# Attention scores as three products of high and low parts, a value product with the values held still, and rotary tables made later, in a two-block network on one core

## The chip, the core and the metric

The program runs on one core of a Trainium2 chip, as one launch. Its engines are TensorE (PE: matrix products; PEld is its loading of the stationary operand), VectorE (DVE), ScalarE (ACT), GpSimd (POOL) and SyncE (SP, which issues most DMAs). The metric is the device time of one execution in microseconds (us), smaller is better.

## What is computed

The reference has two blocks on 256 latent tokens of width 1024, and 256 context tokens beside them in block 1. Everything is float32.

```
block 1, layers l = 0, 1:
    sh, sc, gt ... = ada_modulation(cond, w_ada[l], b_ada[l])
    p  = modulate(rms_norm(h)) @ w_in[l];  pc = the same for the context tokens
    y_a = differential attention: 4 heads; for both 64-wide halves m of a head
            s[m] = q[m] @ k[m].T / 8;  w = softmax(s[0]) - lam * softmax(s[1]);  o = w @ v (128 wide); rms_norm
    y_b = spatial gating
    y_c = neighbourhood attention: 8 heads of 64; window scores + bias and context scores,
            one softmax over both;  o = p @ v
    h  = h + gt1 * (sum over the 3 branches of sigmoid(gate) * (y @ w_branch)) @ w_out
    (layer 0 does all of this for the context tokens too)
    h  = h + gt2 * mixture of 32 experts, 2 a token
block 2:
    gated linear attention, short convolution, dilated attention (q and k rotated by cos/sin of
    positions * inverse frequencies), gated merge, then a feed-forward part
```

## The kernel before

A tile framework takes the program's operations in the order of the code, with their data dependences and buffers, and its scheduler lays down one list of instructions per engine; each engine then works its list in order. So an instruction that waits holds up all that stands behind it on its engine, and where an operation stands is decided when the program is built.

Dense layers take their weights from HBM (2 MB a load, issued by SP into buffers called `raw`), split each into a high part `wh` (ACT copy, L153) and a low part `wl` (DVE subtraction, L155) in the format fp32r, and form three products (`dense_x`: L247 to L249, activations `xh`, `xl` stationary; `dense_w`: L229 to L231, weights stationary). A product of f32 operands is two records of PE in the trace, one of fp32r operands is one.

One call of `mix` handles a layer. Rows of q and k are transposed (`T`, L137) so that features stand on partitions; `qT` and `kT` have 4 tiles of 128 features, and the two 64-row halves of such a tile are the two maps of one differential head, or two neighbourhood heads.

- Differential part: for each of the 128-token tiles `t` (4 in layer 0, 2 in layer 1) and each of 4 heads, two f32 score products (L618), each on its row half of PE; a chain of maximum (L621), exponential (L624), reciprocal and scaling (L626 to L629) on DVE and ACT; 4 or 2 transposes; an ACT copy to `wT` (the transposed weights); and the value product (L637).
- Neighbourhood part: for each tile and each pair of heads two f32 score products (L675), then per head bias and maximum (L689, L691), exponentials (L694, L696), transposes, copy to `wT` (L708) and the value product (L710) with `wT` stationary and 64 columns of v moving. The sum of the exponentials divides the result at the end (L713), and `to_yT` transposes that for the next dense layer (L137, tile `ytok`).

The latent tiles see 512 keys, the context tiles 256. In both parts `at` holds the tiles, with two buffers of `P`/`PC` and four of the tag `t2`; scores, transposes and value products go through the PSUM buffers `aux`. Between one head's scores and its transposes the scheduler puts dense products of the gates or of the modulation vectors of later stages (L361, the modulation products). `gate_branch` and `to_yT` follow.

`rope_tables` (L1336 and on) makes cosT and sinT of block 2 from the inverse frequencies and the positions; before, `idle` calls it at the program's start, behind the norm's scaling (L424), and a table load of ACT stands on either side of it (L1359, L1733). `mix2_consts` makes `sin2`, the table with its negative, and `ev_rope` uses both.

Of the kernel before, what the change touches and what calls it, by code (L numbers as in the profile page):

```python
# [89 lines left out]
class Builder:  # L90
# [173 lines left out]
    def setup(self, st, open_mix, load_x):  # L264
        nc, I = self.nc, self.I
# [6 lines left out]
        c = self.p_const  # L272
# [15 lines left out]
        with self.tp("setup", 1) as tp:  # L288
# [4 lines left out]
            inv = self.p_h.tile([128, 64], FT, name="inv2")  # L293
            nc.gpsimd.dma_start(inv, I["k_inv"])
            pi = self.p_h.tile([128, 2], I32, name="pi")
            nc.gpsimd.dma_start(pi, I["positions_2"][0].rearrange("(t p) -> p t", p=128))
            self.rope_in = inv, pi
# [110 lines left out]
    def mix_norm(self, tp, l, h, mid=None, junk=None, idle=None):  # L408
# [6 lines left out]
        for w in range(2):  # L415
            y = tp.tile([128, 2, D], FT, name="xs", tag="xs", bufs=2)
            r = self.stats(h, (2 * w, 2 * w + 1), y[:, 0] if junk is None else junk)
            if w == 0 and self.spare:
                self.fence.append(self.sq)
            for k in range(2):  # L420
                scaled = nc.vector.tensor_scalar(y[:, k], h[:, 2 * w + k], r[:, k:k + 1], None, op0=OP.mult)
            xs.append(y)
        if idle is not None:
            with self.tc.issue_after(scaled.ins):  # L424
                idle()
# [81 lines left out]
    def mix(self, l, xh, xl):  # L507
# [80 lines left out]
        rope = at.tile([128, 256], FT, name="rope")  # L588
        nc.gpsimd.dma_start(rope, I["k_rope"])

        def ev_qk(dst):
            def ev(t, ps):
# [8 lines left out]
                nc.scalar.activation(dst[:, :, t * 128:(t + 1) * 128], pt.rearrange("p (c t) -> p c t", c=4), AF.Copy)  # L601
# [5 lines left out]
        for t in tts:  # L607
# [4 lines left out]
            for h in range(4):  # L612
                S = [self.aux() for _ in range(2)]
                mx, nm, sm = (self.small(2, f"da{x}") for x in "xns")
                P = at.tile([128, 2, 512], FT, name="P", tag="P", bufs=2)
                for m in range(2):
                    r0 = m * 64
                    mm(S[m][:, :nk], lhsT=qT[r0:r0 + 64, h, t * 128:(t + 1) * 128], rhs=kT[r0:r0 + 64, h, k0:],  # L618
                       start=True, stop=True)
# [3 lines left out]
                for m in range(2):  # L623
                    nc.scalar.activation(P[:, m, :nk], S[m][:, :nk], AF.Exp, bias=nm[:, m:m + 1], scale=0.125,  # L624
                                         accum_out=sm[:, m:m + 1])
# [34 lines left out]
        self.dense_w(W(O_KC), 8, 512, xh, xl, 512, lambda c, ps: nc.scalar.activation(kT[:, c], ps, AF.Copy))  # L660
        self.dense_w(W(O_QC), 8, 512, xh, xl, n, lambda c, ps: nc.scalar.activation(qT[:, c, :n], ps[:, :n], AF.Copy))
        self.dense_x(W(O_VC), 8, 512, xh, xl, allt, lambda t, ps: nc.scalar.activation(v[:, t], ps, AF.Copy))
        yc = at.tile([128, 4, 512], FT, name="ytok", tag="ytok")
        for t in tts:
            po = self.aux()
            sm = self.small(8, "nsm")
# [3 lines left out]
            for h in range(8):  # L670
                c, r0 = h // 2, (h % 2) * 64
                if h % 2 == 0:
                    S2 = [self.aux() for _ in range(2)]
                    for m in range(2):
                        mm(S2[m][:, :nk], lhsT=qT[m * 64:m * 64 + 64, c, t * 128:(t + 1) * 128],  # L675
                           rhs=kT[m * 64:m * 64 + 64, c, k0:], start=True, stop=True)
                S = S2[h % 2]
                P = at.tile([128, 2, 512], FT, name="PC", tag="P", bufs=2)[:, 0]
                mx, nm, ps2 = (self.small(2, f"na{x}") for x in "xns")
                if lat:  # L680
                    if h % 2 == 0:
                        bt = at.tile([128, 2, 4, 64], FT, name="bt", tag="t2", bufs=4)
                        for u in range(2):
                            off = h * 889 + (3 - (2 * t + u)) * 127 + 63
                            for k in range(2):
                                nc.gpsimd.dma_start(bt[u * 64:(u + 1) * 64, k], bass.AP(
                                    tensor=self.d_bias.tensor, offset=self.d_bias[l].offset + off + k * 889,
                                    ap=[[7111, 64], [127, 4], [1, 64]]))
                    nc.vector.tensor_tensor_reduce(P[:, :256], S[:, :256], bt[:, h % 2].rearrange("p a b -> p (a b)"),  # L689
                                                   1.0, -3e38, OP.add, OP.max, mx[:, 0:1])  # L690
                    nc.vector.tensor_reduce(mx[:, 1:2], S[:, 256:], axis=AX.X, op=OP.max)  # L691
                    nc.vector.tensor_tensor(mx[:, 0:1], mx[:, 0:1], mx[:, 1:2], op=OP.max)
                    nc.vector.tensor_scalar(nm[:, 0:1], mx[:, 0:1], -0.125, None, op0=OP.mult)
                    nc.scalar.activation(P[:, :256], P[:, :256], AF.Exp, bias=nm[:, 0:1], scale=0.125,  # L694
                                         accum_out=ps2[:, 0:1])
                    nc.scalar.activation(P[:, 256:], S[:, 256:], AF.Exp, bias=nm[:, 0:1], scale=0.125,  # L696
                                         accum_out=ps2[:, 1:2])
                    nc.vector.tensor_tensor(sm[:, h:h + 1], ps2[:, 0:1], ps2[:, 1:2], op=OP.add)
                else:
                    nc.vector.tensor_reduce(mx[:, 0:1], S[:, :nk], axis=AX.X, op=OP.max)  # L700
                    nc.vector.tensor_scalar(nm[:, 0:1], mx[:, 0:1], -0.125, None, op0=OP.mult)
                    nc.scalar.activation(P[:, :nk], S[:, :nk], AF.Exp, bias=nm[:, 0:1], scale=0.125,
                                         accum_out=sm[:, h:h + 1])
                pt = self.aux()
                for b in range(nk // 128):
                    self.T(pt[:, b * 128:(b + 1) * 128], P[:, b * 128:(b + 1) * 128])
                wT = at.tile([128, 512], FT, name="wT", tag="t2", bufs=4)
                nc.scalar.activation(wT[:, :nk], pt[:, :nk], AF.Copy)  # L708
                for b in range(nk // 128):
# [1125 lines left out]
```

## Time and profile before

| | |
|---|---|
| median of 3 runs | 2613.09 us (2610.91 to 2614.15) |
| the profiled execution | 2611.69 us, its span 2609.9 us |
| PE, DVE, ACT busy over the span | 2471.3 (95%), 1309.2 (50%), 852.0 (33%) us |
| attention of layer 0, layer 1 | 183 to 560 us, 1285 to 1496 us |
| experts of layer 0, layer 1 | 700 to 1175 us, 1560 to 2010 us |
| block 2 | from about 2010 us |

A matrix product's record shows a start and a modelled length; since products are pipelined, the distance from one start to the next is the time that one takes, not the length shown. "x4" in a timeline is four records in a row, "[2.08 <-ACT PC]" is PE's idle time before it and what ended that.

### The profile page before, as it was taken

The numbers are of one execution on the slowest core, as the hardware profiler recorded it, in microseconds if no ns is written. First come the engines' busy times: TensorE is split into PE (matmuls) and PEld (weight loads), VectorE is DVE, ScalarE is ACT, GpSimd is POOL, SyncE is SP. The second block draws the span as 40 slices with busy tenths as digits, with TensorE's granted clock in tenths as the row PEclk, the third lists the DMA queues.
The fourth block names the chain that finished last, engine by engine and source line by source line (L and its number), as shares of the span: only waits on it lengthen the run. The fifth ranks groups of instructions, "written<-read, shape, count | busy, mean of one in ns | idle before, by whom it ended". The sixth has DMA issues, their size and how long they took to land. (4 is left out here: it accounts for less than half of the span.)

```text
span 2609.9 us, 33466 instructions
## 1 busy us (share of the span) xinstructions
PE 2471.3 (95%) x13560; PEld 1686.8 (65%) x13560; DVE 1309.2 (50%) x2640; ACT 852.0 (33%) x1504; POOL 163.2 (6%) x187
## 2 busy tenths in 40 slices
PE   7999999999889999997999978999898899998998
PEld 5766776677544444545878774444342798897997
DVE  5635523346444444548553463233232686657784
ACT  4334333424211111115444441111110534444663
POOL 1200002011200000003000210000000100001000
PEclk9999999999899999998999999999999999999999
DMA  9743544263889999985243478999999435535452
GB/s 316 214 162 114 169 146 122 93 209 149 329 342 417 419 417 418 418 356 193 73 133 104 139 300 328 421 421 421 421 421 413 164 119 194 177 122 184 152 188 99
DMA packets 177363, 652.47 MB, mean 250 GB/s; under 512 B 15174, under 2 KB 18778, under 8 KB 127666
## 3 DMA queue, kind: packets, MB, share of 16 engines
q1 hardware_dynamic: 169682, 626.97, 62.4%
q0 software_dynamic: 7520, 23.29, 3.0%
q8 instruction: 109, 1.79, 0.3%
q14 instruction: 52, 0.43, 0.0%
HBM read 644.42 MB, written 5.80 MB: 249 GB/s over the span
## 5 line engine op out<-in xcount | busy, mean ns | idle before, releaser
L155 DVE TENSOR_TENSOR wl<-raw,wh 128x1024 fp32r<-128x1024 f32 (+1 forms) x279 | 335.8, 1207 | 310.9 <-ACT wh L153 305.3
L966 PE MATMUL acc<-raw,xg 128*64 128x512 f32 x896 | 399.0, 596 | 19.6 <-DMA raw<-in_moe_w_up 10.1
L153 ACT ACTIVATE wh<-raw 128x1024 fp32r<-128x1024 f32 (+1 forms) x288 | 299.0, 1045 | 334.9 <-PE acc L248 167.3
L968 PE MATMUL acc<-raw,xg 128*64 128x512 f32 x896 | 399.2, 596 | 0.0
L247 PE MATMUL acc<-xh,wh 128*128 128x256 f32 (+1 forms) x1184 | 370.6, 315 | 0.0
L248 PE MATMUL acc<-xl,wh 128*128 128x256 f32 (+1 forms) x1184 | 369.5, 313 | 0.0
L249 PE MATMUL acc<-xh,wl 128*128 128x256 f32 (+1 forms) x1184 | 368.5, 312 | 0.1
L966 PEld LDWEIGHTS acc<-raw,xg 128*64 128x64 f32 x896 | 119.8, 137 | 273.4 <-issue 247.2
L247 PEld LDWEIGHTS acc<-xh,wh 128*128 128x128 f32 x1184 | 226.3, 192 | 28.1 <-issue 13.8
L248 PEld LDWEIGHTS acc<-xl,wh 128*128 128x128 f32 x1184 | 226.4, 191 | 15.8 <-issue 5.9
L249 PEld LDWEIGHTS acc<-xh,wl 128*128 128x128 f32 x1184 | 225.9, 191 | 11.7 <-issue 1.0
L229 PE MATMUL acc<-wh,xh 128*128 128x512 f32 x544 | 214.0, 394 | 5.0 <-DVE xh L441 2.5
L230 PE MATMUL acc<-wl,xh 128*128 128x512 f32 x544 | 213.6, 393 | 0.3 <-DVE wl L155 0.3
L231 PE MATMUL acc<-wh,xl 128*128 128x512 f32 x544 | 213.8, 394 | 0.0
L990 PE MATMUL acc<-raw,hT 128*64 128x512 f32 x472 | 209.8, 596 | 3.0 <-ACT hT L982 3.0
L992 PE MATMUL acc<-raw,hT 128*64 128x512 f32 x472 | 209.8, 596 | 0.0
L997 DVE TENSOR_TENSOR aux<-aux,g 128x512 f32<-128x512 f32 x128 | 83.3, 694 | 185.7 <-PE aux L1083 185.7
L1108 DVE SCALAR_TENSOR_TENSOR yl<-acc,ws,yh 128x512 fp32r<-128x512 f32 x64 | 48.0, 750 | 214.6 <-ACT yh L1107 214.6
L990 PEld LDWEIGHTS acc<-raw,hT 128*64 128x64 f32 x472 | 61.8, 137 | 122.7 <-issue 115.3
L982 ACT ACTIVATE hT<-aux 128x512 f32<-128x512 f32 x32 | 19.1, 598 | 332.3 <-PE aux L137 332.3
L229 PEld LDWEIGHTS acc<-wh,xh 128*128 128x128 f32 x544 | 102.4, 188 | 31.8 <-issue 3.7
L968 PEld LDWEIGHTS acc<-raw,xg 128*64 128x64 f32 x896 | 119.8, 137 | 0.0
(479 smaller groups left out, 4303.0 us busy)
## 6 DMA issues: line engine op xcount, KB each, us to landing
raw<-in_moe_w_gate SPq DMA_DIRECT2D x59, 2048.0 KB
raw<-in_moe_w_down SPq DMA_DIRECT2D x59, 2048.0 KB
raw<-in_moe_w_up SPq DMA_DIRECT2D x53, 2048.0 KB
raw<-in_w_in SPq DMA_DIRECT2D x42, 2048.0 KB
raw<-in_w_ada SPq DMA_DIRECT2D x22, 2048.0 KB
rawx<-in_moe_w_up SPq DMA_DIRECT2D x11, 2048.0 KB
raw<-in_w_branch SPq DMA_DIRECT2D x18, 1024.0 KB
raw<-in_w_gate SPq DMA_DIRECT2D x6, 2048.0 KB
```

The source lines that it names most:

```text
L153: nc.scalar.activation(hi, src, AF.Copy)
L155: eng.tensor_tensor(lo, src, hi.bitcast(FT), op=OP.subtract)
L229: mm(ps[t][:, :W], lhsT=a, rhs=wh[:, jj, :W], start=j == 0, stop=False)
L230: mm(ps[t][:, :W], lhsT=a, rhs=wl[:, jj, :W], start=False, stop=False)
L231: self.last_mm = mm(ps[t][:, :W], lhsT=b, rhs=wh[:, jj, :W], start=False, stop=j == J - 1)
L247: mm(ps[c][:, :n], lhsT=a, rhs=xh[:, j, :n], start=j == 0, stop=False)
L248: mm(ps[c][:, :n], lhsT=a, rhs=xl[:, j, :n], start=False, stop=False)
L249: mm(ps[c][:, :n], lhsT=b, rhs=xh[:, j, :n], start=False, stop=j == J - 1)
L966: mm(ps[0:64], lhsT=xg[:, j, a0:a0 + 64], rhs=wa(j), start=j == 0, stop=j == 7)
L968: mm(ps[64:128], lhsT=xg[:, j, b0:b0 + 64], rhs=wb(j), start=j == 0, stop=j == 7)
L990: mm(py[half][0:64], lhsT=hT[:, c, 0:64], rhs=da(c, half), start=c == 0, stop=c == 3)
L992: mm(py[half][64:128], lhsT=hT[:, c, 64:128], rhs=db(c, half), start=c == 0, stop=c == 3)
```

## The change

Four things are changed. The scores of both parts are no longer one f32 product: q and k are kept as high and low fp32r parts (`hilo`: ACT copy, DVE subtraction), and `scores` forms qh·kh, ql·kh and qh·kl, with the two row halves taking turns inside each product. A fence (`scored`) lets the scores of a head or pair issue only when the last exponential of the one before has been issued. In the neighbourhood part v is stationary (64 columns) and the 128 columns of `wT` move; the two heads of a pair write the lower and the upper 64 partitions of the result. The weights are divided by their sum before they are transposed, and the result needs no transposes; an ACT copy and `hilo` take their place. The rotary tables, their inputs and their ACT table load move from the start to block 2, behind the transposes of the linear attention's output; `sin2`'s two DVE operations become a third sine. And the scratch for descriptors of POOL's DMAs is given as 2048 (it was not given), which makes its ring shorter and leaves room for the new tiles.

```diff
         def attn_tiles():
-            return (at.tile([128, 4, 512], FT, name="qT", tag="qT"),
-                    at.tile([128, 4, 512], FT, name="kT", tag="kT"))
+            return [[at.tile([128, 4, k], FR, name=f"{x}{p}", tag=f"{x}{p}") for p in "hl"]
+                    for x, k in (("q", n), ("k", 512))]
 
+        scored = []
+        def scores(c, t, k0):
+            S = [self.aux() for _ in range(2)]
+            nk = 512 - k0
+            with ExitStack() as es:
+                if scored:
+                    es.enter_context(tc.issue_after(scored.pop().ins))
+                for i, (a, b) in enumerate(((0, 0), (1, 0), (0, 1))):
+                    for m in range(2):
+                        r = slice(m * 64, m * 64 + 64)
+                        mm(S[m][:, :nk], lhsT=qT[a][r, c, t * 128:(t + 1) * 128], rhs=kT[b][r, c, k0:],
+                           start=i == 0, stop=i == 2)
+            return S
...
-                nc.scalar.activation(dst[:, :, t * 128:(t + 1) * 128], pt.rearrange("p (c t) -> p c t", c=4), AF.Copy)
+                self.hilo(*(d[:, :, t * 128:(t + 1) * 128] for d in dst), pt.rearrange("p (c t) -> p c t", c=4))
...
-                S = [self.aux() for _ in range(2)]
+                S = scores(h, t, k0)
...
-                for m in range(2):
-                    r0 = m * 64
-                    mm(S[m][:, :nk], lhsT=qT[r0:r0 + 64, h, t * 128:(t + 1) * 128], rhs=kT[r0:r0 + 64, h, k0:],
-                       start=True, stop=True)
...
+                scored[:] = [e]
...
-        self.dense_w(W(O_KC), 8, 512, xh, xl, 512, lambda c, ps: nc.scalar.activation(kT[:, c], ps, AF.Copy))
+        ev = lambda dst, k: lambda c, ps: self.hilo(dst[0][:, c], dst[1][:, c], ps[:, :k])
+        self.dense_w(W(O_KC), 8, 512, xh, xl, 512, ev(kT, 512))
...
-            for h in range(8):
+            for c in range(4):
+                S2 = scores(c, t, k0)
...
+                    scored[:] = [e]
+                    nc.vector.reciprocal(ps2[:, 0:1], ps2[:, 0:1])
+                    nc.vector.tensor_scalar(P[:, :nk], P[:, :nk], ps2[:, 0:1], None, op0=OP.mult)
...
-                for b in range(nk // 128):
-                    mm(po[:, h * 64:(h + 1) * 64], lhsT=wT[:, b * 128:(b + 1) * 128],
-                       rhs=v[:, k0 // 128 + b, h * 64:(h + 1) * 64], start=b == 0, stop=b == nk // 128 - 1)
-            nc.vector.reciprocal(sm, sm)
-            nc.vector.tensor_tensor(yc[:, t].rearrange("p (h d) -> p h d", h=8), po.rearrange("p (h d) -> p h d", h=8),
-                                    sm[:, :, None].to_broadcast([128, 8, 64]), op=OP.mult)
+                for b in range(nb):
+                    for m in range(2):
+                        h = 2 * c + m
+                        mm(po[m * 64:m * 64 + 64, c * 128:(c + 1) * 128],
+                           lhsT=v[:, k0 // 128 + b, h * 64:(h + 1) * 64], rhs=wTs[m][:, b * 128:(b + 1) * 128],
+                           start=b == 0, stop=b == nb - 1)
+            nc.scalar.activation(yc[:, :, t * 128:(t + 1) * 128], po.rearrange("p (c q) -> p c q", c=4), AF.Copy)
...
-        yh, yl = self.to_yT(yc, n)
+        yh = self.p_y.tile([128, 4, n], FR, name="yh", tag="yh")
+        yl = self.p_y.tile([128, 4, n], FR, name="yl", tag="yl")
+        for c in range(4):
+            self.hilo(yh[:, c], yl[:, c], yc[:, c, :n])
...
-        self.sin2 = bp.tile([128, 2, 2, 64], FT, name="sin2")
-        nc.vector.tensor_scalar(self.sin2[:, :, 0], self.rope2[1], -1.0, None, op0=OP.mult)
-        nc.vector.tensor_copy(self.sin2[:, :, 1], self.rope2[1])
...
-        nc.scalar.activation(sinT, a, AF.Sin)
+        nc.scalar.activation(sinT[:, :, 1], a, AF.Sin)
+        nc.scalar.activation(sinT[:, :, 0], a, AF.Sin, scale=-1.0)
...
+        cosT, sinT = self.rope_tables(dl, self.inv, self.pos)
...
-                def idle():
-                    self.rope2 = self.rope_tables(hp, *self.rope_in)
-
-                    nc.scalar.activation(hp.tile([128, 1], FT, name="tab"), self.rope2[0][:, 1, 0:1], AF.Tanh)
...
-    nc = bacc.Bacc("TRN2", target_bir_lowering=False, num_devices=1)
+    nc = bacc.Bacc("TRN2", target_bir_lowering=False, num_devices=1, dynamic_dma_scratch_size=2048)
```

The first place is PE's list in the differential part of layer 0: P is a head's weights, which `glob` (it holds the identity) transposes, `vv` the values, kT and qT the keys and queries, `acc` a dense product. Before:

```order
L249 MATMUL acc<-xh,wl 128x512
L137 MATMUL aux<-glob,P 128x128 x4
L618 MATMUL aux<-kT,qT 128x512
L637 MATMUL aux<-vv,wT 128x128 x4
L618 MATMUL aux<-kT,qT 128x512
L247 MATMUL acc<-xh,wh 128x512
```

After, at the same head, with the parts kh, kl, qh, ql:

```order
L249 MATMUL acc<-xh,wl 128x512
L137 MATMUL aux<-glob,P 128x128 x4
L593 MATMUL aux<-kh,qh 128x512 x2
L593 MATMUL aux<-kh,ql 128x512 x2
L642 MATMUL aux<-vv,wT 128x128 x4
L593 MATMUL aux<-kl,qh 128x512 x2
L247 MATMUL acc<-xh,wh 128x512
```

Two score products with the value product between them have become six, in a group of four and a group of two, around the same value product.

The second place is PE's list in the neighbourhood part of layer 0 (PC is a head's weights). Before:

```order
L137 MATMUL aux<-glob,PC 128x128 x2
L675 MATMUL aux<-kT,qT 128x512
L710 MATMUL aux<-vv,wT 128x64 x4
L675 MATMUL aux<-kT,qT 128x512
L710 MATMUL aux<-vv,wT 128x64 x4
L249 MATMUL acc<-xh,wl 128x512
```

After:

```order
L137 MATMUL aux<-glob,PC 128x128 x4
L721 MATMUL aux<-wT,vv 64x128
L593 MATMUL aux<-kh,qh 128x512 x2
L593 MATMUL aux<-kh,ql 128x512
L721 MATMUL aux<-wT,vv 64x128 x7
L593 MATMUL aux<-kh,ql 128x512
L593 MATMUL aux<-kl,qh 128x512 x2
L249 MATMUL acc<-xh,wl 128x512
```

The value products of a pair stand as one and seven, and the scores of the next pair as three and three around the seven.

The third place is PE's list at the end of the neighbourhood part of layer 1. Before (the first three rows are the last of 29 dense products in a row):

```order
L247 MATMUL acc<-xh,wh 128x256
L248 MATMUL acc<-xl,wh 128x256
L249 MATMUL acc<-xh,wl 128x256
L137 MATMUL aux<-glob,PC 128x128 x4
L710 MATMUL aux<-vv,wT 128x64 x4
L137 MATMUL aux<-glob,PC 128x128 x2
L137 MATMUL aux<-glob,ytok 128x128
```

After:

```order
L249 MATMUL acc<-xh,wl 128x256
L137 MATMUL aux<-glob,PC 128x128 x8
L721 MATMUL aux<-wT,vv 64x128
L593 MATMUL aux<-kh,qh 128x512
L721 MATMUL aux<-wT,vv 64x128 x7
L593 MATMUL aux<-kh,qh 128x512
L593 MATMUL aux<-kh,ql 128x512 x2
L593 MATMUL aux<-kl,qh 128x512 x2
L137 MATMUL aux<-glob,PC 128x128 x8
L721 MATMUL aux<-wT,vv 64x128 x8
L247 MATMUL acc<-yh,wh 128x256 x4
```

The last pair's scores now come behind the dense products, with no dense product between them and the last pair's transposes, and the transposes of the result (ytok) are gone.

## Rows read from the trace of the kernel before

**Rows 1.** Stretches: start:end, length, busy us (records) by engine, PEclk, DMA share, GB/s.

```profile
180.00:270.00 90.00, 89.15 (x408) 54.70 (x408) 49.92 (x126) 37.75 (x93) 1.50 (x3) 1.00 0.30 103
380.00:480.00 100.00, 99.65 (x487) 64.19 (x486) 35.78 (x123) 41.57 (x106) 16.37 (x27) 1.00 0.36 110
700.00:1175.00 475.00, 465.04 (x2377) 227.18 (x2374) 212.29 (x394) 57.23 (x92) 0.00 (x0) 0.99 0.97 399
1480.00:1500.00 20.00, 16.18 (x85) 13.15 (x84) 6.73 (x21) 7.96 (x20) 4.48 (x7) 0.77 0.55 173
2120.00:2290.00 170.00, 169.97 (x1029) 151.32 (x1028) 111.29 (x162) 77.71 (x98) 0.00 (x0) 1.00 0.51 171
```

**Rows 2.** Waits of PE, whole span: tile <- releaser: us, times, longest.

```profile
PE aux L137 <- ACT PC L694: 2.9, 3, 2.1
PE aux L137 <- DVE P L629: 2.5, 7, 0.6
```

**Rows 3.** Lines L675 (scores) and L710 (values): records, ns min/median/max, forms.

```profile
L675 PE MATMUL aux<-kT,qT x96: 376/589/694, 382.7 to 1482.7; 64*128 64x512 f32 x64, 64*128 64x256 f32 x32
L710 PE MATMUL aux<-vv,wT x320: 217/275/473, 388.8 to 1495.7; 128*128 128x64 f32 x160
```

**Rows 4.** PE's timeline, a pair of row halves: start, us, line, names, form, records.

```profile
183.38 1.13 PE L618 MATMUL aux<-kT,qT 64*128 64x512 f32 x4
```

**Rows 5.** PE's timeline, one row half alone.

```profile
200.32 0.72 PE L637 MATMUL aux<-vv,wT 128*128 128x128 f32 x5
200.97 1.12 PE L618 MATMUL aux<-kT,qT 64*128 64x512 f32 x2
202.03 0.50 PE L247 MATMUL acc<-xh,wh 128*128 128x512 f32 x1
202.36 0.39 PE L248 MATMUL acc<-xl,wh 128*128 128x512 f32 x1
202.59 0.39 PE L249 MATMUL acc<-xh,wl 128*128 128x512 f32 x1
```

**Rows 6.** PE's timeline, value product of the neighbourhood part.

```profile
412.91 2.00 PE L710 MATMUL aux<-vv,wT 128*128 128x64 f32 x16
414.84 1.12 PE L675 MATMUL aux<-kT,qT 64*128 64x512 f32 x2
```

**Rows 7.** Timeline, a pair of column halves in the expert part (PEld loads weights).

```profile
1667.28 0.59 PE L966 MATMUL acc<-rawx,xg 128*64 128x512 f32 x1
1667.28 0.14 PEld L966 LDWEIGHTS acc<-rawx,xg 128*64 128x64 f32 x1 [0.29 <-issue]
1667.28 0.59 PE L968 MATMUL acc<-rawx,xg 128*64 128x512 f32 x1
...
1667.70 0.59 PE L966 MATMUL acc<-rawx,xg 128*64 128x512 f32 x1
```

**Rows 8.** PE's timeline, from scores to transposes, differential part of layer 1.

```profile
1346.36 0.50 PE L247 MATMUL acc<-xh,wh 128*128 128x512 f32 x1
...
1350.69 0.63 PE L137 MATMUL aux<-glob,P 128*128 128x128 f32 x4
```

**Rows 9.** Timeline, end of the neighbourhood part of layer 1.

```profile
1486.52 0.28 PE L248 MATMUL acc<-xl,wh 128*128 128x256 f32 x1
...
1486.64 0.28 PE L249 MATMUL acc<-xh,wl 128*128 128x256 f32 x1
...
1488.35 0.50 ACT L694 ACTIVATE PC<-PC,nan 128x256 f32<-128x256 f32 x1
...
1494.17 1.97 PE L710 MATMUL aux<-vv,wT 128*128 128x64 f32 x8 [0.47 <-ACT wT L708]
...
1497.91 0.78 PE L247 MATMUL acc<-yh,wh 128*128 128x256 f32 x2
```

**Rows 10.** Timeline, modulation part at the start.

```profile
17.16 3.11 PE L361 MATMUL acc<-raw,condT 128*32 128x512 f32 x16
...
20.53 0.58 ACT L366 ACTIVATE part<-acc 128x512 f32<-128x512 f32 x1
```

More of the change, by code (lines that the diff above doesn't have):

```diff
@@ L406, in stats, with mix_norm @@
         return self.rsqrt(ss, 1.0 / D, EPS)
-    def mix_norm(self, tp, l, h, mid=None, junk=None, idle=None):
+    def mix_norm(self, tp, l, h, mid=None, junk=None):
         nc = self.nc
@@ L420, in mix_norm @@
             for k in range(2):
-                scaled = nc.vector.tensor_scalar(y[:, k], h[:, 2 * w + k], r[:, k:k + 1], None, op0=OP.mult)
+                nc.vector.tensor_scalar(y[:, k], h[:, 2 * w + k], r[:, k:k + 1], None, op0=OP.mult)
             xs.append(y)
-        if idle is not None:
-            with self.tc.issue_after(scaled.ins):
-                idle()
         order = [(w, j) for w in range(2) for j in range(0, 8, 2)]
@@ L712, in mix @@
-            nc.vector.reciprocal(sm, sm)
-            nc.vector.tensor_tensor(yc[:, t].rearrange("p (h d) -> p h d", h=8), po.rearrange("p (h d) -> p h d", h=8),
-                                    sm[:, :, None].to_broadcast([128, 8, 64]), op=OP.mult)
-            self.dump(f"yc{l}", lambda o: o[t * 128:(t + 1) * 128], yc[:, t])
+            nb = nk // 128
+            for c in range(4):
+                S2 = scores(c, t, k0)
+                if lat:
+                    bt = at.tile([128, 2, 4, 64], FT, name="bt", tag="t2", bufs=4)
+                    for u in range(2):
+                        off = 2 * c * 889 + (3 - (2 * t + u)) * 127 + 63
+                        for k in range(2):
+                            nc.gpsimd.dma_start(bt[u * 64:(u + 1) * 64, k], bass.AP(
+                                tensor=self.d_bias.tensor, offset=self.d_bias[l].offset + off + k * 889,
+                                ap=[[7111, 64], [127, 4], [1, 64]]))
+                wTs = []
+                for m in range(2):
+                    S = S2[m]
+                    P = at.tile([128, 2, 512], FT, name="PC", tag="P", bufs=2)[:, 0]
+                    mx, nm, ps2 = (self.small(2, f"na{x}") for x in "xns")
+                    if lat:
+                        nc.vector.tensor_tensor_reduce(P[:, :256], S[:, :256], bt[:, m].rearrange("p a b -> p (a b)"),
+                                                       1.0, -3e38, OP.add, OP.max, mx[:, 0:1])
+                        nc.vector.tensor_reduce(mx[:, 1:2], S[:, 256:], axis=AX.X, op=OP.max)
+                        nc.vector.tensor_tensor(mx[:, 0:1], mx[:, 0:1], mx[:, 1:2], op=OP.max)
+                        nc.vector.tensor_scalar(nm[:, 0:1], mx[:, 0:1], -0.125, None, op0=OP.mult)
+                        nc.scalar.activation(P[:, :256], P[:, :256], AF.Exp, bias=nm[:, 0:1], scale=0.125,
+                                             accum_out=ps2[:, 0:1])
+                        e = nc.scalar.activation(P[:, 256:], S[:, 256:], AF.Exp, bias=nm[:, 0:1], scale=0.125,
+                                                 accum_out=ps2[:, 1:2])
+                        nc.vector.tensor_tensor(ps2[:, 0:1], ps2[:, 0:1], ps2[:, 1:2], op=OP.add)
+                    else:
+                        nc.vector.tensor_reduce(mx[:, 0:1], S[:, :nk], axis=AX.X, op=OP.max)
+                        nc.vector.tensor_scalar(nm[:, 0:1], mx[:, 0:1], -0.125, None, op0=OP.mult)
+                        e = nc.scalar.activation(P[:, :nk], S[:, :nk], AF.Exp, bias=nm[:, 0:1], scale=0.125,
+                                                 accum_out=ps2[:, 0:1])
+                    scored[:] = [e]
+                    nc.vector.reciprocal(ps2[:, 0:1], ps2[:, 0:1])
+                    nc.vector.tensor_scalar(P[:, :nk], P[:, :nk], ps2[:, 0:1], None, op0=OP.mult)
+                    pt = self.aux()
+                    for b in range(nb):
+                        self.T(pt[:, b * 128:(b + 1) * 128], P[:, b * 128:(b + 1) * 128])
+                    wT = at.tile([128, 512], FT, name="wT", tag="t2", bufs=4)
+                    nc.scalar.activation(wT[:, :nk], pt[:, :nk], AF.Copy)
+                    wTs.append(wT)
+                for b in range(nb):
+                    for m in range(2):
+                        h = 2 * c + m
+                        mm(po[m * 64:m * 64 + 64, c * 128:(c + 1) * 128],
+                           lhsT=v[:, k0 // 128 + b, h * 64:(h + 1) * 64], rhs=wTs[m][:, b * 128:(b + 1) * 128],
+                           start=b == 0, stop=b == nb - 1)
@@ L1336, in rope_tables @@
     def rope_tables(self, rp, inv, pi):
-        nc, I, c = self.nc, self.I, self.p_const
-        cosT = c.tile([128, 2, 64], FT, name="cosT")
-        sinT = c.tile([128, 2, 64], FT, name="sinT")
+        nc = self.nc
+        cosT = rp.tile([128, 2, 64], FT, name="cosT")
+        sinT = rp.tile([128, 2, 2, 64], FT, name="sinT")
         pf = rp.tile([128, 2], FT, name="pf")
```

59 lines of the change are left out of this document (10 added, 49 removed).

## The prediction, made before the changed kernel ran

> **What bounds the kernel now.** I read the table of stretches first, then PE's waits, then the two score and value lines, and last the timelines around them. In the stretches the reader is to see that PE has next to no idle time while the attention runs: 89.15 of 90 us and 99.65 of 100 us, with DVE at about half and ACT at 40% [rows 1]. The waits say the same from the other side: over the whole program PE waits 2.9 and 2.5 us for the two softmax chains [rows 2]. So dense products of other stages cover the softmax, and what a stage there costs is the sum of what PE does in it: time taken out of PE's list shortens it one for one, as long as the chain stays covered. The experts are another case: DMA share 0.97 and 399 GB/s over 475 us [rows 1]. They wait for weights, but these are loaded into the buffers that the attention and its gates still hold, and in the attention the DMA is idle two thirds of the time (share 0.30 and 0.36 [rows 1]), so the weight stream starts earlier when the attention ends earlier, and the gain is kept.
>
> **What the rows price.** A record of an f32 product with 512 columns takes 0.42 to 0.43 us (start to start, 1667.28 to 1667.70 [rows 7]), a product has two, so 0.853. An fp32r product of 512 columns takes 0.23 (202.36 to 202.59 [rows 5]; 0.2275 over longer runs), one of 256 columns 0.12 (1486.52 to 1486.64 [rows 9]). Two row halves that stand next to each other run at once: four records last 1.13 us [rows 4], two records of one half alone last 1.12 [rows 5].
>
> Going into a row half and out of it costs. The half alone holds PE from 200.97 to 202.03, 1.06, which is 0.853 and 0.2; the five value records of 128 columns before it take 0.65, where a quarter of 0.4275 each would make 0.53, 0.1 too much; the first dense product behind it takes 0.33 instead of 0.23 [rows 5]. That is 0.4 for a group, 0.2 for each of its two boundaries. [...]
>
> **Scores.** Each of the two lines has 64 records at 512 columns and 32 at 256 [rows 3], together 64 products of 512 and 32 of 256. In PE's order of before, 24 of the 512 stand in 12 pairs and 40 alone, of the 256 also 12 pairs and 8 alone. So PE holds 52 turns of 0.853 and 20 of 0.427 (half): 44.4 + 8.5 = 52.9 us. After, there are three times as many products, 288, in 90 groups of one to six; two halves in a group share a turn, which gives 107 turns at 512 and 54 at 256: 107 × 0.2275 + 54 × 0.12 = 24.3 + 6.5 = 30.8. That is −22.1. No row of before shows fp32r on row halves. If they run one after the other, it is 192 × 0.2275 + 96 × 0.12 = 55.2, +2.3. I take the first, since f32 halves run at once in [rows 4] and the format is not what places them.
>
> **Value product of the neighbourhood part.** 320 records [rows 3], sixteen in 1.93 us [rows 6], 0.1206 each: 38.6 us. After, 160 f32 products of 128 moving columns with 64 stationary ones, in two column halves. Column halves of f32 run at once in the experts: both start at 1667.28 and the next at 1667.70 [rows 7]. A record of 128 columns takes a quarter of that 0.4275, 0.107; I take 0.112, near the 0.12 that records with a 128-column load reach. By the order (runs of one and seven, eight, three) the 160 make 101 turns: 101 × 0.224 = 22.6, −16.0. If the halves don't share a turn, it is 160 × 0.224 = 35.8, −2.8.
>
> **Transposes and boundaries.** 24 transposes of the result go (16 in layer 0, 8 in layer 1), at about 0.12: −2.9. In exchange ACT copies and splits the result; that work falls where dense products of gate 1 stand, except in layer 1 (below). About 29 changes between dense products and transposes go, since the transposes now stand as four, and some score groups beside modulation products: −2. The boundaries into and out of split groups rise from 144 to 206, as the value products are now split as well and stand between the scores: 62 × 0.2 = +12.4; it can be nothing where two kinds of split follow each other, so between 0 and 12.4, and I take it whole.
>
> PE's list becomes 22.1 + 16.0 + 2.9 + 2 − 12.4 = 30.6 us shorter, 30.
>
> **Waits that it adds.** The fence lets a pair's scores issue only behind the last exponential of the pair before. What is queued behind waiting scores is PE's whole list, the dense products too. In the differential part the scores stand behind the transposes anyway, which need that exponential; between scores and transposes PE has 21 to 23 dense products of 512 columns, 4.8 to 5.2 us, while the chain took 4.33 us (1346.36 to 1350.69 [rows 8]) with one maximum already at work; with both behind the scores it is some 0.6 longer. So it is just covered; +1 in all. In the neighbourhood part of layer 0 the latent pairs have 26 to 30 dense products, 5.9 to 6.8 us, and the chain gets two more DVE operations for a head, +1.5; the context pairs have 8 to 12, 1.8 to 2.7 us, for a chain with one exponential: +2 over eight pairs.
>
> At the end of layer 1 the last pair has no cover. [...] From the first exponential to the second head's value product it took 5.82 us (1488.35 to 1494.17 [rows 9]). After, the dense products stand ahead of the last pair's scores and cover the pair before by 3.4 of its 6, and the last pair's chain runs bare: about 0.9 for its maxima, 5.8, 0.9 for the new scaling and 3 for values, copy and split, 10.6 where it was 11.2, and 2.5 to 3.5 for the pair before, less the ytok transposes. I take +4, between 0 and +8.
>
> **Rotary tables.** At the start nothing is won: PE's modulation products (L361) last until 20.27 and ACT reads them at 20.53 [rows 10], so at most 0.26 us lies there. In block 2 PE is busy 169.97 of 170 [rows 1], and the list of ACT gets four pieces (a table load and three sines, 2 us at an exponential's 0.50 [rows 9]) and DVE's fourteen (7 us at most at the same price) ahead of the first rotated q. ACT has 92 and DVE 59 us free there, and PE has the next dense tiles to work on, until its accumulators are full. Between 0 and +7; I take +1. POOL's shorter descriptor ring meets some four small DMAs a pair, off the path: 0. The high and low parts of q and k add a DVE subtraction to an ACT copy per tile, behind which dense products run: 0, within +1.
>
> Waits in sum: 1 + 1.5 + 2 + 4 + 1 = 9.5, I take 8 to 9, since some of PE's 5.4 us of waits [rows 2] go at the same time. Net −22. The profiled execution took 2611.7 us, 1.4 below the median 2613.1; against its own time that is 2590, against the median **2591 us**.
>
> **Rivals.**
> [...]
> - *fp32r halves run one after the other*: the scores give +2.3 instead of −22.1: 2615, no change. Against it speaks the f32 pair of [rows 4].
> [...]
> - *Slower: the softmax chain comes bare.* With the fence only one pair is in flight on 48 pairs and heads; where a weight split of ACT or DVE is queued between its maximum and its exponential, PE stands. The 30 us of the shorter list are gone from 0.62 us a pair; at 1.2, one split each, it is 58 − 30 = +28: 2641. For it: ACT did put two splits ahead of the exponential at 1488.35 and PE waited there [rows 9]. Against: the dense products in the list were placed to cover the chain, by count they do.
> - *The weight stream swallows it*: if the experts' weights came no earlier, 2611. Against it is the idle DMA in the attention.
>
> **Chances.** The forecast with its own range, 2580 to 2602: 0.63. Cheaper boundaries 0.13. Halves in turn 0.07, of which half no change and half a little faster. Loads not hidden 0.03. Stream 0.03. Slower by a bare chain 0.11. A change below 0.2% (5 us) can't be told from none. Faster 0.63 + 0.13 + 0.03 = 0.79; same 0.04 + 0.015 + 0.03, 0.085; slower 0.11 + 0.015, 0.125. For 8 in 10 the range takes the forecast, the cheaper boundaries and the start of the weaker cases: 2567 to 2613.
>
> **What would show it.** Right: score records of 0.23 with equal starts for two halves, value records in pairs at 0.11 to 0.12; the start of the experts of layer 0 some 14 to 18 us earlier, of layer 1 a further 5 to 9; PE's waits for the chains up from 5 to about 14 us, most at the end of layer 1's neighbourhood part. Wrong: halves with starts 0.23 apart; value records at 0.2 or more; long waits of PE on PC or P in every pair; or an attention that ends earlier and experts that don't.

## The result and the profile after

| | before | after |
|---|---|---|
| median | 2613.62 us (4 runs, 2610.91 to 2615.92) | 2579.31 us (4 runs, 2577.66 to 2579.85) |
| profiled execution, its span | 2611.69, 2609.9 us | 2577.66, 2575.9 us |
| first score product of layer 0 | 183.38 | 176.04 |
| first score product of the neighbourhood part | 382.71 | 369.86 |
| first expert product of layer 0 | 690.29 | 663.98 |
| first score product of layer 1, of its neighbourhood part | 1286.34, 1404.10 | 1259.50, 1374.35 |
| first expert product of layer 1 | 1573.48 | 1539.65 |

The ratio is 0.9868, interval 0.9851 to 0.9885: 34 us faster, where 22 were forecast. The time lies inside the range given for 8 in 10 (2567 to 2613) and 0.7 us below the likeliest case's own (2580 to 2602). By stages, from the starts in the table: 7.3 us are won at the start, 5.5 and 13.5 in the two parts of layer 0, 2.9 and 4.1 in those of layer 1, each taken with what follows it up to the next start. From the first expert product of layer 0 to the scores of layer 1, and from the first expert product of layer 1 to the end, both kernels take the same time to about 0.5 us.

The stretches again, of the changed kernel (columns as in [rows 1]; the last two are moved with their stages):

```profile
180.00:270.00 90.00, 89.07 (x455) 62.59 (x455) 49.63 (x132) 39.35 (x97) 1.50 (x3) 1.00 0.33 116
380.00:480.00 100.00, 99.28 (x553) 66.26 (x551) 45.79 (x160) 44.80 (x116) 15.16 (x26) 1.00 0.40 130
...
1445.00:1466.00 21.00, 11.96 (x66) 8.09 (x65) 8.02 (x28) 10.23 (x28) 4.48 (x7) 0.76 0.45 136
2085.00:2255.00 170.00, 169.97 (x1032) 151.65 (x1031) 113.33 (x174) 82.67 (x103) 0.00 (x0) 1.00 0.52 176
```

PE is as full in the attention as before [rows 1], so the gain is time taken out of its list. The exception is the end of layer 1's neighbourhood part, 11.96 of 21 us. PE's waits for the softmax chains say where (answers to [rows 2]):

```profile
PE aux L137 <- ACT PC L699: 3.7, 1, 3.7
PE aux L137 <- ACT PC L701: 3.4, 1, 3.4
...
PE aux L137 <- DVE P L634: 0.4, 2, 0.2
```

The first two rows are one wait each, both at that end. In the differential part (the third row) the waits went down, from 2.5 [rows 2] to 0.4 us.

PE's timeline around a group of six score products and its value product in the differential part (answers to [rows 4, 5]):

```profile
185.10 1.08 PE L642 MATMUL aux<-vv,wT 128*128 128x128 f32 x8
186.12 0.49 PE L593 MATMUL aux<-kh,qh 64*128 64x512 f32 x2
186.45 0.39 PE L593 MATMUL aux<-kh,ql 64*128 64x512 f32 x2
186.68 0.40 PE L593 MATMUL aux<-kl,qh 64*128 64x512 f32 x2
187.01 0.50 PE L248 MATMUL acc<-xl,wh 128*128 128x512 f32 x1
187.34 0.40 PE L249 MATMUL acc<-xh,wl 128*128 128x512 f32 x1
```

Each row of two records is one turn of both halves. From start to start a turn takes 0.33 (the first one), 0.23 and 0.33 us (the last one), and the first dense product behind it 0.33 instead of 0.23. The six products take 0.89 us; the same scores took 1.06 as a pair [rows 4] and 2.1 as two singles [rows 5].

The end of layer 1's neighbourhood part (answers to [rows 9]; the last of the dense products first):

```profile
1445.57 0.28 PE L249 MATMUL acc<-xh,wl 128*128 128x256 f32 x1
1449.52 0.70 PE L137 MATMUL aux<-glob,PC 128*128 128x128 f32 x4 [3.67 <-ACT PC L699]
1450.92 1.09 PE L137 MATMUL aux<-glob,PC 128*128 128x128 f32 x4 [0.71 <-ACT wT L716]
1451.94 0.69 PE L721 MATMUL aux<-wT,vv 128*64 128x128 f32 x2
...
1455.77 1.05 PE L593 MATMUL aux<-kl,qh 64*128 64x512 f32 x2
1460.22 2.03 PE L137 MATMUL aux<-glob,PC 128*128 128x128 f32 x8 [3.40 <-ACT PC L701]
1462.18 2.18 PE L721 MATMUL aux<-wT,vv 128*64 128x128 f32 x16
1465.49 0.74 PE L247 MATMUL acc<-yh,wh 128*128 128x256 f32 x4 [1.13 <-ACT yh L161]
```

It is 19.9 us from the last dense product to the next branch where it was 11.3 [rows 9], with two pairs in it instead of the rest of one. The granted clock of the stretch is 0.76: taken by the microsecond it was 1.00 until 1449, 0.50 from 1450 to 1456, 1.00 from 1457 to 1460, 0.50 from 1461 to 1463 and 1.00 from 1464 on. The 0.77 of [rows 1] was 1.00 until 1490 and 0.50 from 1491 to 1500.

At the start, two waits of PE that were not in the forecast are gone. Here they are in PE's timeline of before, and below them what POOL and DVE did ahead of the first:

```profile
50.98 0.50 PE L229 MATMUL acc<-wh,xh 128*128 128x512 f32 x1 [2.45 <-DVE xh L441]
...
134.84 0.50 PE L229 MATMUL acc<-wh,xh 128*128 128x512 f32 x1 [2.43 <-ACT row L386]
```

```profile
47.59 3.06 POOL L339 MEMSET merged<- 64x3556 f32 x1 [30.25 <-PE aux L137]
48.18 2.75 DVE L441 CAST xh<-xm 128x512 fp32r<-128x512 f32 x1 [0.45 <-ACT xm L439]
```

The fill and the conversion in the changed kernel:

```profile
42.37 3.06 POOL L334 MEMSET merged<- 64x3556 f32 x1 [26.30 <-PE aux L356]
...
47.44 0.43 DVE L433 CAST xh<-xm 128x512 fp32r<-128x512 f32 x1
```

POOL's fill of the bias buffer ran beside DVE's conversion, which ended 0.28 us behind it (50.93 and 50.65). Now the fill runs 5 us earlier, and the conversion takes 0.43 us instead of 2.75. The second wait, for ACT's `row`, goes back to a 4 KB DMA (`brow`): DVE's sum waited for its landing, and the next `row` waited for the sum. Before:

```profile
133.43 0.68 DVE L389 TENSOR_TENSOR row<-row,brow 2x512 f32<-2x512 f32 x1 [5.83 <-DMA brow<-in_b_ada]
```

Behind that wait, from 135.6 to 139.0 us, PE's products stand 0.43 us apart instead of 0.23; the granted clock is 1.00 until 135, 0.50 from 136 to 139 and 1.00 again from 140. The wait and that stretch cost some 4 us. Both waits of PE are absent after. By the same dense products in both lists PE is 0.7 us ahead at 29 us, 3.1 at 48, 3.3 at 125 and 7.3 at 137.

### The profile page after: what moved, and what is told of

It is laid out like the page before. It is cut to its first block, busy times and chain, and to the rows that moved or that the text cites. A ratio compares the mean times of both kernels' runs of the same rounds, so it can differ in the third digit from the quotient of the medians.

```text
span 2575.9 us, 33740 instructions
## 1 busy us (share of the span) xinstructions
PE 2438.7 (95%) x13632; PEld 1670.3 (65%) x13632; DVE 1340.3 (52%) x2752; ACT 855.1 (33%) x1510; POOL 162.7 (6%) x187
## 5 line engine op out<-in xcount | busy, mean ns | idle before, releaser
L153 ACT ACTIVATE wh<-raw 128x1024 fp32r<-128x1024 f32 (+1 forms) x288 | 299.8, 1047 | 339.4 <-PE acc L248 176.3
```

The costliest lines, as they stand in the source:

```text
L153: nc.scalar.activation(hi, src, AF.Copy)
```

## Experiments

Times and ratios are against runs of the kernel before on the same chip. The changed kernel was run on another occasion, so a difference from it, or from e5, is one of two medians and can be off by about 2 us: by the ratios e5 is 10 us below it instead of 11.7, and e8 12 above it instead of 9.8. A trace is of one execution.

**e1, the tables alone.** Before, with the parts of the diff on `rope_tables`, its inputs, `idle` and `sin2`, and nothing else.

> Before, with the rotary tables alone moved to block 2 (scores, values and POOL's descriptor scratch as before). Theory A (the 7.4 us that the changed kernel is ahead at its first score product come from the moved tables and what their going shifts at the start): 2613.6 - 7 = 2606 us, PE's two waits of 2.4 and 2.5 us before 184 us gone, block 2 unchanged. Rival B (the start won because the rest of the change shifted instructions, such as the fill of POOL's buffer): 2611 to 2614, both waits still there. Rival C (the tables cost something in block 2 that the start pays for): first scores some 7 us earlier but block 2 longer by 1 to 7 us, 2607 to 2613.

Measured: 2608.65 us, ratio 0.9986 (0.9976 to 0.9995), 4.5 us faster where theory A had 7. The fill ran at 42.24 and the wait for xh was gone; the wait for row stayed (2.8), so that half of theory A failed. First scores stand at 178.6 instead of 183.4, and from the first to the last score product each part of the attention takes the same time to 0.3 us. From the last expert product to the end, which is block 2, it is 583.7 us (before 582.9, the changed kernel 582.8): theory C's 1 to 7 us are not there, 0.8 at most.

**e2, the descriptor scratch alone.** `+ dynamic_dma_scratch_size=2048` on before.

> Before, with the descriptor scratch of POOL's DMAs alone set to 2048. Theory A (the shorter ring meets nothing on the path): 2613.6 within 2 us. Rival B (the shorter ring lets POOL's small DMAs wait, or changes their landing): a change of over 3 us, visible as POOL's or DVE's waits on bt, gbc or brow.

Measured: 2612.14 us, 0.9997 (0.9987 to 1.0006): no change. Both waits at the start stay (2.5 and 2.7). The scratch does show in POOL's issues, with nothing waiting behind them: the router's second load now comes 3.49 us after the first, where it came 0.91 after it before (1483.56 and 1484.47).

```profile
1482.30 0.91 POOL L786 DMA_DIRECT2D wr<-in_moe_w_router  x1 [10.22 <-PE aux L675]
1485.79 0.89 POOL L787 DMA_DIRECT2D wr<-in_moe_w_group  x1 [2.58 <-issue]
```

**e3, e9, e12, the fill.** Three edits of before: the fill at the setup; the fill held by a fence; and a one-column copy on POOL that depends on the norm's last result, ahead of the fill.

```diff
+                    nc.gpsimd.tensor_copy(pad[:, 0, 0, 0:1], self.xl_last.bitcast(FT))
                     nc.gpsimd.memset(pad, NEG)
```

> Before, with POOL's fill of the bias buffer (merged, 3.06 us at 47.59) moved to the program's start; PE's list is the same. Theory A (the 2.45 us that PE waits for xh at 51 us come from DVE's conversion running 2.75 instead of 0.43 us beside POOL's fill): that wait gone, conversion back at 0.43, 2613.6 - 2.3 = 2611.3. Rival B (the conversion was late for another reason): conversion still over 2 us, 2613.6.

> Before, with POOL's fill of the bias buffer (3.06 us) held until the norm's last subtraction has been issued; the lists of PE and DVE are the same. In e3 the fill stood earlier in the program but waited for its buffer until 48.16, beside the same conversion, so that run told nothing. Theory A (DVE's conversion to xh runs 2.75 instead of 0.43 us because POOL fills beside it): the 2.5 us wait of PE for xh at 51 us gone, 2613 - 2.4, about 2610.5, or the same slowing on another DVE operation later. Rival B (the conversion is late for another reason): it still takes over 2 us.

> Before, with a one-column copy on POOL that reads the norm's last result (xl) put ahead of the fill of the bias buffer, so that the fill can only start behind it; the scheduler lays later stages a little otherwise for it, so the first 60 us are what is compared. Theory A (DVE's conversion to xh takes 2.75 us because POOL fills beside it): the conversion that took 2.75 takes 0.43, PE's wait of 2.5 us for xh is gone, the fill runs from about 52 to 55 us, where it may slow another operation of DVE; 2610 to 2612. Rival B (that conversion waits for something else, such as PE's transposes): 2.75 again, with the fill behind it.

Measured: e3 2612.05 (0.9994, 0.9985 to 1.0004) and e9 2612.18 (0.9999, 0.9990 to 1.0009), and in both the fill ran where it had run, at 48.16 and 47.12, behind a wait for PE's transposes as before, with the conversion at 2.75: neither edit moved it, so they don't decide between the theories. In e12 it moved. POOL first, then DVE:

```profile
53.05 0.23 POOL L339 COPY merged<-xl 64x1 f32<-64x1 f32 x1 [35.82 <-DVE xl L443]
53.35 3.07 POOL L340 MEMSET merged<- 64x3556 f32 x1
```

```profile
48.05 0.43 DVE L442 CAST xh<-xm 128x512 fp32r<-128x512 f32 x1 [0.44 <-ACT xm L440]
```

The wait for xh is gone; the wait for row stays (2.8). 2609.14, 0.9984 (0.9974 to 0.9993); that is 4.3 us, and what it holds beyond the 2.4 of the wait isn't shown. Theory A is shown for the conversion: it took 2.75 us beside the fill and 0.43 without it.

**e4 and e5, cover for the end of layer 1.** The changed kernel, with both gate halves of the last branch ahead of its branch products (in layer 1 only), and for e5 also the router's loads in another order.

```diff
-            self.dense_w(br_src[:, half * 512:(half + 1) * 512], 4, 512, yh, yl, n, ev_br)
+            late.append(lambda half=half, ev=ev_br: self.dense_w(br_src[...], 4, 512, yh, yl, n, ev))
+            if not early or half == 1:
+                for f in late:
+                    f()
+                late = []
```

> The changed kernel, with the last branch of layer 1 forming both halves of its gate ahead of its two branch products (a second buffer G). 96 dense products of 256 columns that need no attention result then stand in PE's list between the last scores and transposes (60 and 52 instead of 28 and 0). Theory A (the end of layer 1's neighbourhood part stands bare and costs what its waits and its half clock show, 19.8 us from the last dense product to the next branch of which 7 to 8 are work at full speed): 2579.3 - 8, about 2571 (2569 to 2574), the waits on PC of 3.7 and 3.4 us gone. Rival B (the weights of the experts or of the gates arrive no earlier, so the wait moves behind): 2577 to 2580.

Measured: 2578.68, 0.9866 (0.9849 to 0.9882): no gain over the changed kernel's 0.9868. That is rival B's number, by another wait than the weights. The end is covered (PE 91.29 of 91.60 us busy up to 1466), but a new wait of 7.7 us, for the modulation rows `cr`, stands behind it. PE's row and then POOL's:

```profile
1503.34 0.28 PE L137 MATMUL aux<-glob,cr 32*128 32x32 f32 x1 [7.70 <-DMA cr<-d_rows]
```

```profile
1487.00 0.92 POOL L804 DMA_DIRECT2D wr<-in_moe_w_router  x1
1498.14 0.89 POOL L805 DMA_DIRECT2D wr<-in_moe_w_group  x1 [10.22 <-issue]
...
1500.10 0.53 POOL L810 DMA_DIRECT2D cr<-d_rows  x1
```

> The kernel of e4 with the router's small loads in another order: the modulation rows cr ahead of the router's weights, and the tile hm behind them. In e4 the bare end of layer 1 was gone (PE 91.29 busy of 91.60 us), but PE then waited 7.7 us for cr, which stood on POOL behind a load of the router that was issued 11 us after the one before it. Theory A (the end of the neighbourhood part was worth 7 to 8 us and e4 gave them back on cr alone): no wait on cr, 2579.3 - 7.5, about 2572 (2569 to 2575). Rival B (the experts' weights set the pace from there): no wait on cr, but longer waits for in_moe_w_up or w_gate, 2577 to 2580.

Measured: 2567.6, 0.983 (0.9817 to 0.9844), 11.7 us below the changed kernel's median; no wait on cr. From the first score of the neighbourhood part to the experts layer 1 takes 153.8 instead of 165.3 us. That is theory A's cause, with 11.5 for the bare end where 7.5 was expected. Rival B falls.

**e6, e7, the two products apart.** The changed kernel with f32 scores; and with the value product of before.

```diff
-                for i, (a, b) in enumerate(((0, 0), (1, 0), (0, 1))):
+                for i, (a, b) in enumerate(((0, 0),)):
```

> The changed kernel with one f32 product for each score, as before the change, and everything else of the change. Theory A (the scores' three fp32r products win by their turns): 53 turns of 0.853 and 21 of 0.427 instead of 110 of 0.2275 and 60 of 0.12 is +22.0, 27 boundaries of 0.2 fewer is -5.4: +16.6, 2596 (2591 to 2600). Rival B (the scores are hidden, the gain is the start's and the value product's): 2579 to 2584.

> The changed kernel with the value product of before (weights stationary, division at the end, transposes of the result), and everything else of the change. Theory A: 160 products at 0.241 instead of 103 turns at 0.224 is +15.5, transposes and their changes +4.9, 34 boundaries of 0.2 fewer -6.8, score turns -1.8, the shorter chain and the end of layer 1 with more cover -2 to -4: +8 to +12, 2588 to 2591. Rival B (the stationary values win nothing, since their boundaries eat it): 2577 to 2583.

Measured: e6 2601.35 (0.9954, 0.9939 to 0.9969), 22 above the changed kernel; about 4 of it are the wait for row, which the profiled execution had (2.7; first scores at 180.5), so 18 against the 16.6 expected. Some 2 of the 18 are waits on P, which are back at 2.5 us. Rival B falls. e7 2586.43 (0.99, 0.9885 to 0.9915), 7.1 above the changed kernel: just under theory A's 2588 to 2591, and above rival B's 2577 to 2583. Only the neighbourhood part of layer 0 is longer, 303.0 instead of 294.1 us to the experts, while layer 1 is level, where PE's waits on PC are 2.8 instead of 7.1 us. So the stationary values do win in layer 0, and in layer 1 the bare end eats it.

**e8, the order of the halves.** The changed kernel with the two loops of `scores` exchanged.

```diff
-                for i, (a, b) in enumerate(((0, 0), (1, 0), (0, 1))):
-                    for m in range(2):
+                for m in range(2):
+                    for i, (a, b) in enumerate(((0, 0), (1, 0), (0, 1))):
```

> The changed kernel with the three products of one row half ahead of the three of the other, so that neighbours in PE's list are of the same half. Theory A (that the two halves run at once is what makes three products cheap): 190 turns of 512 and 96 of 256 instead of 110 and 60, +22.5; where the third product of one half runs beside the first of the other, a sixth to a quarter less; 8 boundaries fewer -1.6: +15 to +21, 2594 to 2600. Rival B (the format alone makes the gain, halves run at once wherever they stand): 2578 to 2582.

Measured: 2589.12, 0.9915 (0.9899 to 0.993): 9.8 slower than the changed kernel, between the two theories. The trace shows why. In a whole group PE's products now stand, by the order of the code:

```
L593 MATMUL aux<-kh,qh 128x512
L593 MATMUL aux<-kh,ql 128x512
L593 MATMUL aux<-kl,qh 128x512
L593 MATMUL aux<-kh,qh 128x512
L593 MATMUL aux<-kh,ql 128x512
L593 MATMUL aux<-kl,qh 128x512
```

and that group ran as

```profile
186.23 0.50 PE L593 MATMUL aux<-kh,qh 64*128 64x512 f32 x2
...
186.56 0.39 PE L593 MATMUL aux<-kh,ql 64*128 64x512 f32 x2
...
186.79 0.39 PE L593 MATMUL aux<-kl,qh 64*128 64x512 f32 x2
```

The fourth product of the list started with the first (186.23 and 186.24), ahead of the second and third. So each half took its own products in order and did not wait for the other: a group costs its longer half. (A record doesn't name its row half; that PE's list keeps the order of the code shows in the broken group below, whose first piece has one half's three products and one of the other's.) What e8 lost it lost in broken groups, as four and two with three of one half in the first piece:

```profile
201.50 0.51 PE L593 MATMUL aux<-kh,qh 64*128 64x512 f32 x2
201.83 0.39 PE L593 MATMUL aux<-kh,ql 64*128 64x512 f32 x1
202.07 0.39 PE L593 MATMUL aux<-kl,qh 64*128 64x512 f32 x1
202.38 1.16 PE L642 MATMUL aux<-vv,wT 128*128 128x128 f32 x8
203.47 0.49 PE L593 MATMUL aux<-kh,ql 64*128 64x512 f32 x1
203.81 0.39 PE L593 MATMUL aux<-kl,qh 64*128 64x512 f32 x1
```

Five turns instead of three. Over all, groups have 215 turns instead of 167 by the starts in the trace. By the distance from a group's first product to whatever follows it, the groups take 64.4 us instead of 57.1, 7.3 more; 2.2 more are waits on P (2.6 instead of 0.4).

**e10, e11, unbroken groups.** e5 with the next scores ahead of this pair's value product in the code, and that product issued behind the last of them; in e11 for the neighbourhood part alone, with `brow` loaded ahead of the weights.

```diff
+            if pend:
+                with tc.issue_after(last.ins):
+                    pend.pop()()
...
-                for b in range(nb):
+                def values(t=t, c=c, wTs=wTs, k0=k0, nb=nb):
...
+                pend.append(values)
```

> The kernel of e5, with the six score products of the next pair or head ahead of the value product of this one, in one group, and the value product directly behind them. Theory A (a boundary of a split group costs 0.2 us, a broken turn a whole turn): 128 instead of 207 boundaries -15.8, score turns -1.8, 80 instead of 103 value turns -5.2: -22.8; in the differential part of layer 0 only 16 dense products stand between scores and transposes, 3.6 us for a chain of 5, up to +8 of waits: 2567.6 - 19, about 2549 (2544 to 2555). Rival B (going from one kind of split to another costs nothing, only the way in and out of whole-array work does): some 40 of the boundaries that go are of that kind, -8 less: 2553 to 2560. Rival C (the chain was covered by the broken groups, and the waits come back in every pair): 2562 or more.

> The kernel of e5, with the scores in one group ahead of the value product in the neighbourhood part alone (the differential part as in e5), and the 4 KB rows of modulation bias (brow) issued on SP ahead of the 2 MB weight load of their stage. Theory A: 156 instead of 207 boundaries -10.2, turns -1.8 and -5.2, no wait for row at the start -0 to -3: 2567.6 - 18, about 2549 (2545 to 2554), no waits on P in the differential part. Rival B (the wait for row is not the place of its DMA in the queue): the wait for row is there again, 2.2 to 2.8 us.

Measured: e10 2544.06, 0.9738 (0.9724 to 0.9751), 23.5 below e5 (21 by the two traces) and 35 below the changed kernel. That is theory A, with hardly a wait in the differential part (0.7 us on P in all). A pair in PE's timeline:

```profile
391.77 0.63 PE L137 MATMUL aux<-glob,PC 128*128 128x128 f32 x4
392.33 0.50 PE L604 MATMUL aux<-kh,qh 64*128 64x512 f32 x2
392.67 0.39 PE L604 MATMUL aux<-kh,ql 64*128 64x512 f32 x2
392.90 0.39 PE L604 MATMUL aux<-kl,qh 64*128 64x512 f32 x2
393.23 1.09 PE L746 MATMUL aux<-wT,vv 128*64 128x128 f32 x16
394.25 0.50 PE L247 MATMUL acc<-xh,wh 128*128 128x512 f32 x1
```

e11 2561.29, 0.98 (0.9786 to 0.9814), 6 below e5 instead of 18. The neighbourhood parts are 6.3 and 4.8 us shorter, 11.1 where the sum had 17.2, and the start is 9 us longer (first scores at 185.3 instead of 176.3). SP's waits and ACT's `row` at the start show why:

```profile
SPq L354 <- DVE row L385: 18.0, 3, 9.8
```

```profile
134.38 0.59 ACT L384 ACTIVATE row<-acc 2x512 f32<-2x512 f32 x1 [9.43 <-DMA d_rows<-row]
```

`brow` and `row` share two buffers (tag `row`). A `brow` that is loaded early holds one of them: SP waits for a buffer before it can issue `brow`, with the weights' loads behind it, and ACT's next `row` waited 9.43 us, until the row before it had been written out. PE's wait for row was 3.4 us, at 135. So rival B's sign came, but for a reason of this edit's own, and the run doesn't tell whether the place of `brow` in the queue matters.

## Why the prediction was right, and where it was short

*Scores.* By the distance from a group's first product to whatever follows it, the 72 groups of before take 67.5 us; the forecast's 52.9 and 0.2 a group for the way out make 67.3. The 90 of after take 57.1, of which 4.2 are one wait (1455.77 to 1460.22): 52.9, where the forecast's terms make 30.8 + 18.0 = 48.8. So the scores won 14.6 where 18.5 were forecast. The mechanism was right (halves run at once, e8), the size 4 short; about 1 of the 4 is turns, 167 instead of the 161 counted. e6 puts the part at 16 to 18.

*Values and transposes.* By the same measure the value products of the neighbourhood part went from 39.4 to 32.3 us, −7.1, with most of those at the end of layer 1 at a granted clock of 0.50; the forecast was 22.6 + 9 = 31.6. The transposes from the first scores of a layer to its experts went from 45.2 to 40.8, −4.4, where the forecast had −4.9.

*Boundaries.* The sum of the three is −26.1, and the value products of the differential part, now beside split groups more often, are 0.9 longer. The forecast had −30.6 with 12.4 for the boundaries taken whole. What makes up the rest isn't in its terms: the dense products between them take 4.9 us less by the same measure, 1.0 of it shorter waits and the rest not taken apart. So PE's list came out 30.1 shorter, close to the forecast, but by luck: 4 too much in the scores against 4.9 that nobody had counted. That the boundaries were taken whole was near the mark in e10, which takes 79 of them and 31 turns away and wins 21 to 23.5, near the 22.8 of its sum; in e11 the same prices gave 17.2 and the parts won 11.1. Cheaper boundaries, 0.13 in the chances, are not what made the larger gain.

*Waits it adds.* This step failed in size. The forecast had 8 to 9; the stages of the attention are 26.0 us shorter and the list 30.1, so 4 were added, the one long wait. In the differential part and in layer 0 none were (0.4 on P where it had been 2.5): I had put 1 + 1.5 + 2 there. The end of layer 1 was the +4 forecast (its 3.4 is 29 dense products at the 0.12 of [rows 9], its 11.2 the time from 1486.64 to 1497.91 there), and e5 shows what all of it is worth: 11.5, of which before had some 7 (an estimate: the 11.3 us of [rows 9] less 16 transposes and 16 value records at 0.12). The rival of a bare chain failed with that: of 48 pairs and heads only the last two pairs of layer 1 stood bare. The rival was built on the fence; no run leaves the fence out, so what it costs by itself isn't shown.

*Rotary tables.* The failed step that is worth most: "At the start nothing is won" (0.26 at most) was argued from the tables' own instructions. What was won is elsewhere: 2.4 us where POOL's fill no longer falls on DVE's conversion (e1, e12), 0.7 by the first dense product at 29 us (PE's wait for its first load, `glob`, is 9.3 us instead of 11.4), and about 4 with the wait for row (2.4) and the clock of 0.50 behind it. That last part is not the change's for sure. In the traces of the five kernels with the tables at the start (before, e2, e3, e9, e12) the wait is there, 2.4 to 2.8 us. Among those that make them in block 2 it is absent in the changed kernel, e5, e8 and e10, 0.2 in e7, and 2.2 to 2.8 in e1, e4 and e6, though e4 and e5 have the same code at the start. It may come and go between executions of one kernel: the four times of e4 go from 2576.54 to 2583.49, and the profiled one, which had the wait, is the slowest. What makes `brow` land late is open. Block 2, where +1 was taken, is unchanged (582.9 and 582.8 us).

So 34 is 26 from the attention, where 22 was forecast, and 7 to 8 at the start; without the wait for row some 30. The sign that the experts of layer 0 would start 14 to 18 us earlier came out as 26, 19 of them from the attention; the further 5 to 9 of layer 1 came out as 7.5.

## What to carry to other kernels

Count the list of a PE that works in halves by turns and boundaries: here a group of half-array products cost its longer half and about 0.2 us at either end, and keeping a pair's scores and values in one unbroken run (e10, 23.5 us) was worth more than the whole change of arithmetic in the scores (16 to 18). When code is moved out of a stage, look at what its buffers and instructions had been keeping in place there, not only at its own time. And a covered chain needs cover in its last member too: work that depends on nothing should be kept for the end.

## What the runs showed of the hardware

- Two row halves took their products independently: with three products of one half ahead of three of the other in the code, the fourth started 10 ns after the first and 0.33 us ahead of the second (e8).
- DVE's conversion of 128x512 took 2.75 us beside POOL's 3.06 us fill and 0.43 without it (e12); a DVE subtraction of 128x1024 that began half a microsecond before the same fill's end in the changed kernel took 1.2 (two in 2.36 from 44.94), where such subtractions took 1.22 on average in the kernel before.
- With the descriptor scratch at 2048, POOL issued the router's second load 11.14 us after the first in e4 and 3.42 in the changed kernel; in e2, where the scratch is the only edit, 3.49, and in the kernel before 0.91. It cost nothing until something waited behind it (the 7.7 us of e4).
